# Contrast adjustment of 48 images: tiles of 64 KB rows in three buffers, loads and stores in one written-out order on one queue, sums shared by VectorE and ScalarE

## Chip, cores, metric

One core of a Trainium2 chip. The metric is device time in microseconds (us), the median over executions. The *span* is the time from the first to the last instruction in one profiled execution.

## The reference

```python
x: (16, 3, 512, 512) float32, uniform in [0, 1);  factor = 1.5
mean = np.mean(x, axis=(2, 3), keepdims=True)
return np.clip(mean + factor * (x - mean), 0, 1).astype(np.float32)
```

Each of the 48 images (262,144 pixels, 1 MB) needs its own mean before any of its pixels can be finished. Everything is read once and written once: 50.33 MB in, 50.33 MB out.

## The kernel before

Tiles of four images (4 MB, 128 partitions with rows of 32 KB), the last two tiles of two images, in five buffers. VectorE sums a row, a matmul with a block matrix adds the partitions of an image and multiplies by (1 - factor)/n, ScalarE computes relu(factor * x + bias), VectorE takes the minimum with 1. Loads are issued from SyncE, stores from GpSimd.

```python
TILE_IMGS = [4] * 11 + [2, 2]
X_BUFS = 5
STORE_ENGINE = "gpsimd"
# ... pools, blockw ...
    for i, N in enumerate(TILE_IMGS):
        # ... FREE = columns of this tile, 8192 or 4096; src, dst ...
        nc.sync.dma_start(out=xt, in_=src)
        nc.vector.tensor_reduce(out=rsum, in_=xt, axis=mybir.AxisListType.X, op=mybir.AluOpType.add)
        nc.tensor.matmul(pbias, blockw[N], rsum, start=True, stop=True)
        nc.scalar.copy(out=bias, in_=pbias)
        nc.scalar.activation(out=xt, in_=xt, func=mybir.ActivationFunctionType.Relu, bias=bias, scale=factor)
        nc.vector.tensor_scalar(out=xt, in0=xt, scalar1=1.0, scalar2=None, op0=mybir.AluOpType.min)
        store_eng.dma_start(out=dst, in_=xt)
```

The framework derives the semaphores: a store waits for the last min, a load for the store that last used its buffer.

## Time and profile before

| | before |
|---|---|
| time, median of the first three executions | 240.48 us |
| span of the profiled execution | 238.6 us |
| traffic | 100.66 MB, mean 422 GB/s |
| the two DMA queues | 49.4% + 49.0% of the 16 DMA engines' time |
| VectorE / ScalarE busy | 66% / 37% |

The page of the profile before. In the rows `DMA` and `GB/s` the span is cut into 40 equal slices of 5.97 us; a digit 9 means that the 16 DMA engines were busy for 90% or more of it. The rows `q1` and `q0` are the two DMA queues: packets, MB, share of the engines' time. A group line ends with busy time, the mean duration of one instruction in ns, and the idle time in front of it.

```profile
span 238.6 us, 238 instructions
PE 7.4 (3%) x26; PEld 6.5 (3%) x26; DVE 156.5 (66%) x26; ACT 89.1 (37%) x27; POOL 10.3 (4%) x25
DMA  7999999999999999999999999999999999999995
GB/s 269 434 439 439 439 439 352 439 434 439 439 439 439 439 434 434 423 428 412 423 439 439 434 439 439 439 439 439 434 428 426 426 404 428 431 434 439 428 434 214
...
q1 hardware_dynamic: 1872, 50.33, 49.4%
q0 software_dynamic: 1872, 50.33, 49.0%
...
L77 DVE TENSOR_REDUCE rsum<-xt 128x1 f32<-128x8192 f32 (+1 forms) x13 | 104.4, 8029 | 61.7 <-DMA xt<-in_x_dram 61.7
L90 ACT ACTIVATE xt<-xt,bias 128x8192 f32<-128x8192 f32 (+1 forms) x13 | 85.8, 6598 | 0.4
L97 DVE TENSOR_SCALAR xt<-xt 128x8192 f32<-128x8192 f32 (+1 forms) x13 | 53.2, 4091 | 5.0 <-ACT xt L90 5.0
```

Neither computing engine is near full; the DMA engines are. The timeline of the kernel before shows their pace where stores leave (start, duration of the issue, what; in brackets how long GpSimd had been idle and what ended it):

```profile
136.95 0.53 POOL L104 DMA_DIRECT2D out_dram<-xt  x1 [18.81 <-DVE xt L97]
156.32 0.53 POOL L104 DMA_DIRECT2D out_dram<-xt  x1 [18.84 <-DVE xt L97]
175.69 0.53 POOL L104 DMA_DIRECT2D out_dram<-xt  x1 [18.83 <-DVE xt L97]
```

One store and one load of 4 MB pass every 19.37 us: 433 GB/s. The whole traffic at that pace is 100.66 MB / 433 GB/s = 232.4 us of the 238.6 us span. So the most that any reordering could gain is the rest, 6 us, and part of that (the start, the last landing) can't go. The Trainium skill, "DMA: Bandwidth & Descriptors", section "Where 436 GB/s comes from", gives 435.2 GB/s as the ceiling of the 16 ports that the DMA engines share; the 433 GB/s of this trace agree.

### The profile page before, as it was taken

The page shows a single profiled execution, that of the slowest core. Times are in us where ns is not written, and L with a number is a line of the kernel's source. Part 1 is how long each engine was busy: PE and PEld are TensorE (multiplying, and loading weights), DVE is VectorE, ACT ScalarE, POOL GpSimd, SP SyncE. Part 2 cuts the span into 40 slices and gives each one's busy share as a digit, 9 for nine tenths or more (in the row PEclk, how much of TensorE's full clock was granted, in tenths as well). Part 3 has the DMA queues.
Part 4 walks back from the last instruction along what each step waited for, and adds up shares of the span by engine and source line. Part 5 has one row for each costly group of instructions (what it writes and reads, how often), then busy time and mean ns, then how long its engine had stood idle before and what let it go on. Part 6 is the DMA issues. An engine that isn't in the chain of part 4 may idle for free.

```text
span 238.6 us, 238 instructions
## 1 busy us (share of the span) xinstructions
PE 7.4 (3%) x26; PEld 6.5 (3%) x26; DVE 156.5 (66%) x26; ACT 89.1 (37%) x27; POOL 10.3 (4%) x25
## 2 busy tenths in 40 slices
PE   0000000000000000000000000000000000000000
PEld 0000000000000000000000000000000000000000
DVE  0088999999599079459629909917945979742300
ACT  2002966472906601900920650470190095406000
POOL 2000001000000000000000000000000000500000
DMA  7999999999999999999999999999999999999995
GB/s 269 434 439 439 439 439 352 439 434 439 439 439 439 439 434 434 423 428 412 423 439 439 434 439 439 439 439 439 434 428 426 426 404 428 431 434 439 428 434 214
DMA packets 3744, 100.66 MB, mean 422 GB/s; under 512 B 416, under 2 KB 416, under 8 KB 416
## 3 DMA queue, kind: packets, MB, share of 16 engines
q1 hardware_dynamic: 1872, 50.33, 49.4%
q0 software_dynamic: 1872, 50.33, 49.0%
HBM read 50.33 MB, written 50.33 MB: 422 GB/s over the span
## 4 chain that ended last, share of the span: by engine, by line
issue 38%; DMA 35%; DVE 18%; POOL 2%; POOLq 0%; SPq 0%
DMA xt<-in_x_dram 19%; DMA out_dram<-xt 16%; DVE rsum L77 11%; DVE xt L97 7%; POOL out_dram L104 2%; POOLq L137 0%; SPq L74 0%; POOLq L104 0%
## 5 line engine op out<-in xcount | busy, mean ns | idle before, releaser
L77 DVE TENSOR_REDUCE rsum<-xt 128x1 f32<-128x8192 f32 (+1 forms) x13 | 104.4, 8029 | 61.7 <-DMA xt<-in_x_dram 61.7
L90 ACT ACTIVATE xt<-xt,bias 128x8192 f32<-128x8192 f32 (+1 forms) x13 | 85.8, 6598 | 0.4
L97 DVE TENSOR_SCALAR xt<-xt 128x8192 f32<-128x8192 f32 (+1 forms) x13 | 53.2, 4091 | 5.0 <-ACT xt L90 5.0
L88 ACT COPY bias<-pbias 128x1 f32<-128x1 f32 x13 | 2.1, 160 | 130.6 <-PE pbias L85 130.6
L104 POOL DMA_DIRECT2D out_dram<-xt x13 | 9.0, 692 | 213.0 <-DVE xt L97 212.8
L85 PE MATMUL pbias<-rsum,blockw 128*128 128x1 f32 x26 | 7.4, 355 | 209.5 <-DVE rsum L77 209.5
L85 PEld LDWEIGHTS pbias<-rsum,blockw 128*128 128x128 f32 x26 | 6.5, 311 | 210.3 <-DVE rsum L77 107.1
L88 ACT ACT_TABLE_LOAD x1 | 1.3, 1283 | 0.8 <-PEq L123 0.8
L51 POOL MEMSET blockw<- 32x32 f32 (+1 forms) x6 | 0.8, 128 | 0.2
L49 POOL MEMSET blockw<- 128x128 f32 x2 | 0.3, 205 | 0.3 <-POOLq L123 0.3
L123 POOL MEMSET const-float32-0.0<- 128x1 f32 x1 | 0.1, 104 | 0.2 <-issue 0.2
L123 POOL MEMSET const-bfloat16-1.0<- 128x1 bf16 x1 | 0.1, 113 | 0.0
L123 POOL MEMSET const-uint8-127<- 128x1 uint8 x1 | 0.1, 113 | 0.0
L123 POOL MEMSET const-float32-1.0<- 128x1 f32 x1 | 0.1, 110 | 0.0
## 6 DMA issues: line engine op xcount, KB each, us to landing
xt<-in_x_dram SPq DMA_DIRECT2D x11, 4096.0 KB, 24.6
out_dram<-xt POOLq DMA_DIRECT2D x11, 4096.0 KB, 36.0
xt<-in_x_dram SPq DMA_DIRECT2D x2, 2048.0 KB, 19.5
out_dram<-xt POOLq DMA_DIRECT2D x2, 2048.0 KB, 19.1
```

The lines of the kernel that those rows point to most:

```text
L49: nc.gpsimd.memset(wt, 0.0)
L51: nc.gpsimd.memset(wt[b * PPI : (b + 1) * PPI, b * PPI : (b + 1) * PPI], wconst)
L77: nc.vector.tensor_reduce(out=rsum, in_=xt, axis=mybir.AxisListType.X, op=mybir.AluOpType.add,)
L85: nc.tensor.matmul(pbias, blockw[N], rsum, start=True, stop=True)
L88: nc.scalar.copy(out=bias, in_=pbias)
L90: nc.scalar.activation(out=xt, in_=xt, func=mybir.ActivationFunctionType.Relu, bias=bias, scale=factor,)
L97: nc.vector.tensor_scalar(out=xt, in0=xt, scalar1=1.0, scalar2=None, op0=mybir.AluOpType.min,)
L104: store_eng.dma_start(out=dst, in_=xt)
L123: nc = _bacc.Bacc("TRN2", target_bir_lowering=False, num_devices=1)
```

## The change

The intent: fewer and larger transfers, one queue with an order chosen by hand so that the DMA engines always have the right transfer next, and a tile's sum in half the time. Tiles of 8 MB (128 rows of 64 KB) need 64 KB per partition, and three buffers of them 192 KB, against 160 KB for the five before. The diff, cut to its core:

```diff
-TILE_IMGS = [4] * 11 + [2, 2]
-X_BUFS = 5
-STORE_ENGINE = "gpsimd"
+P = 128
+ROW = 16384
+BUFS = 3
+HALF = ROW // 2
+CHUNK = 4096
+JUNK = 2048
 ...
+    def load(t):
+        xt = xpool.tile([P, ROW], f32, name="xt")
+        nc.sync.dma_start(out=xt, in_=dram(x_f, t))
+        tiles[t] = xt
+
+    def compute(t):
+        xt = tiles[t]
+        n_act = (ROW - HALF) // JUNK
+        sums = rpool.tile([P, 1 + n_act], f32, name="sums")
         nc.vector.tensor_reduce(
-            out=rsum, in_=xt, ...
+            out=sums[:, 0:1], in_=xt[:, 0:HALF], axis=mybir.AxisListType.X, op=Alu.add
         )
+        for j in range(n_act):
+            junk = jpool.tile([P, JUNK], f32, name="junk")
+            a = HALF + j * JUNK
+            nc.scalar.activation(
+                out=junk, in_=xt[:, a : a + JUNK], func=Act.Copy, accum_out=sums[:, 1 + j : 2 + j]
+            )
+        pbias = psum.tile([P, 1], f32, name="pbias")
+        for j in range(1 + n_act):
+            nc.tensor.matmul(pbias, blockw, sums[:, j : j + 1], start=j == 0, stop=j == n_act)
+        bias = bpool.tile([P, 1], f32, name="bias")
+        nc.scalar.copy(out=bias, in_=pbias)
+        for c in range(0, ROW, CHUNK):
+            part = xt[:, c : c + CHUNK]
+            nc.scalar.activation(out=part, in_=part, func=Act.Relu, bias=bias, scale=factor)
+            nc.vector.tensor_scalar(out=part, in0=part, scalar1=1.0, scalar2=None, op0=Alu.min)
+
+    def store(t):
+        nc.sync.dma_start(out=dram(out_f, t), in_=tiles.pop(t))
+
+    for t in range(min(BUFS, n_tiles)):
+        load(t)
+    compute(0)
+    store(0)
+    compute(1)
+    store(1)
+    load(3)
+    compute(2)
+    store(2)
+    load(4)
+    load(5)
+    for t in (3, 4, 5):
+        compute(t)
+        store(t)
```

Below, L0 to L5 and S0 to S5 are the loads and stores of the six tiles. The queue's order is L0 L1 L2 S0 S1 L3 S2 L4 L5 S3 S4 S5. A *turn* is a place in it where a store follows a load or a load follows a store. *Ring* stands below for the list of transfers that one queue hands to the DMA engines.

More of the change, by code (lines that the diff above doesn't have):

```diff
@@ L5 @@
 import concourse.tile as tile
-from concourse import bass_utils, mybir
+from concourse import mybir
 from concourse._compat import with_exitstack
-TILE_IMGS = [4] * 11 + [2, 2]
-X_BUFS = 5
-STORE_ENGINE = "gpsimd"
+P = 128
[4 more added lines that the diff above has]
+JUNK = 2048
 @with_exitstack
@@ L23 @@
     nc = tc.nc
-    P = 128
+    f32 = mybir.dt.float32
+    Alu = mybir.AluOpType
+    Act = mybir.ActivationFunctionType
     B, C, H, W = x.shape
-    n_img = B * C
-    n_pix = H * W
+    n_img, n_pix = B * C, H * W
+    ppi = n_pix // ROW
+    per_tile = P // ppi
+    n_tiles = n_img // per_tile
+    assert ppi * ROW == n_pix and per_tile * n_tiles == n_img
     factor = float(factor)
-    f32 = mybir.dt.float32
-    assert sum(TILE_IMGS) == n_img
-    NMAX = max(TILE_IMGS)
+    wconst = (1.0 - factor) / float(n_pix)
@@ L36, with dram @@
     x_f = x.rearrange("b c h w -> (b c h w)")
     out_f = out.rearrange("b c h w -> (b c h w)")
-    wconst = (1.0 - factor) / float(n_pix)
+    def dram(ap, t):
+        return bass.AP(tensor=ap.tensor, offset=t * P * ROW, ap=[[ROW, P], [1, ROW]])
     consts = ctx.enter_context(tc.tile_pool(name="consts", bufs=1))
-    blockw = {}
-    for N in sorted(set(TILE_IMGS)):
-        wt = consts.tile([P, P], f32, name=f"blockw{N}")
-        PPI = P // N
-        if N == 1:
-            nc.gpsimd.memset(wt, wconst)
-        else:
-            nc.gpsimd.memset(wt, 0.0)
-            for b in range(N):
-                nc.gpsimd.memset(wt[b * PPI : (b + 1) * PPI, b * PPI : (b + 1) * PPI], wconst)
-        blockw[N] = wt
@@ L54 @@
-    xpool = ctx.enter_context(tc.tile_pool(name="xpool", bufs=X_BUFS))
-    rpool = ctx.enter_context(tc.tile_pool(name="rpool", bufs=12))
-    bpool = ctx.enter_context(tc.tile_pool(name="bpool", bufs=12))
-    psum = ctx.enter_context(tc.tile_pool(name="psum", bufs=8, space=bass.MemoryType.PSUM))
-    if STORE_ENGINE == "sync":
-        store_eng = nc.sync
-    elif STORE_ENGINE == "act":
-        store_eng = nc.scalar
-    else:
-        store_eng = nc.gpsimd
-    pix_off = 0
-    for i, N in enumerate(TILE_IMGS):
-        FREE = n_pix * N // P
-        npix_tile = n_pix * N
-        xt = xpool.tile([P, NMAX * n_pix // P], f32, name="xt")[:, :FREE]
-        src = bass.AP(tensor=x_f.tensor, offset=pix_off, ap=[[FREE, P], [1, FREE]])
-        dst = bass.AP(tensor=out_f.tensor, offset=pix_off, ap=[[FREE, P], [1, FREE]])
-        nc.sync.dma_start(out=xt, in_=src)
-        rsum = rpool.tile([P, 1], f32)
+    xpool = ctx.enter_context(tc.tile_pool(name="xpool", bufs=BUFS))
@@ new lines @@
+    jpool = ctx.enter_context(tc.tile_pool(name="jpool", bufs=1))
+    rpool = ctx.enter_context(tc.tile_pool(name="rpool", bufs=2))
+    bpool = ctx.enter_context(tc.tile_pool(name="bpool", bufs=2))
+    psum = ctx.enter_context(tc.tile_pool(name="psum", bufs=2, space=bass.MemoryType.PSUM))
+    blockw = consts.tile([P, P], f32, name="blockw")
+    nc.gpsimd.memset(blockw, 0.0)
+    for a in range(0, P, 2 * ppi):
+        mid, end = a + ppi, a + 2 * ppi
+        nc.gpsimd.memset(blockw[a:end, mid:end], wconst)
+        nc.gpsimd.memset(blockw[a:mid, mid:end], 0.0)
+        nc.gpsimd.memset(blockw[a:mid, a:mid], wconst)
@@ L77 @@
+    tiles = {}
+    def load(t):
[6 more added lines that the diff above has]
+        sums = rpool.tile([P, 1 + n_act], f32, name="sums")
         nc.vector.tensor_reduce(
-            out=rsum,
-            in_=xt,
-            axis=mybir.AxisListType.X,
-            op=mybir.AluOpType.add,
-        )
-        pbias = psum.tile([P, 1], f32)
@@ L85 @@
-        nc.tensor.matmul(pbias, blockw[N], rsum, start=True, stop=True)
-        bias = bpool.tile([P, 1], f32)
-        nc.scalar.copy(out=bias, in_=pbias)
-        nc.scalar.activation(
-            out=xt,
-            in_=xt,
-            func=mybir.ActivationFunctionType.Relu,
-            bias=bias,
-            scale=factor,
-        )
-        nc.vector.tensor_scalar(
-            out=xt,
-            in0=xt,
-            scalar1=1.0,
-            scalar2=None,
-            op0=mybir.AluOpType.min,
-        )
@@ L104 @@
-        store_eng.dma_start(out=dst, in_=xt)
-        pix_off += npix_tile
+            out=sums[:, 0:1], in_=xt[:, 0:HALF], axis=mybir.AxisListType.X, op=Alu.add
+        )
+        for j in range(n_act):
[5 more added lines that the diff above has]
+        pbias = psum.tile([P, 1], f32, name="pbias")
```

## The prediction

> **What bounds the kernel now: the DMA engines.** The slice row "DMA" stands at 9 from the second slice on, and the two queues hold 49.4% and 49.0% of the 16 engines' time. The kernel must move 100.66 MB. In the middle of the timeline stores are issued exactly every 19.37 us, one 4 MB load plus one 4 MB store each: 8.389 MB / 19.37 us = 433 GB/s. At that rate the traffic alone takes 232.4 us of the 238.6 us span. The Trainium skill, "DMA: Bandwidth & Descriptors", section "Where 436 GB/s comes from", puts the ceiling at 435.2 GB/s; the trace agrees. The rest is about 2.3 us of start (first slice 269 GB/s), 3 us of tail (last slice 214 GB/s), and a small dip, for instance slice 7 at 352 GB/s, where the first store joins. VectorE is busy 66%, ScalarE 37%: not the limit.
>
> **What the change does.** The bytes stay. Stores move from GpSimd's queue to SyncE's; the same skill page, "Issuing engines are not separate DMA queues", says both end on the same 16 engines, so no bandwidth is gained. The dips with two queues may go (about 1 us, at most 4 us if every slice reached 439 GB/s). Tiles double to 8 MB, 19.4 us each on the engines, in the queue order L0 L1 L2 S0 S1 L3 S2 L4 L5 S3 S4 S5. Whether the engines ever run dry depends on how long a tile computes.
>
> Costs from the timeline: reduction of 8192 columns 8.69 us; relu 8192 7.12, 4096 3.71, hence 0.83 ns per column and a 2048 sum about 2.0 (four: 8); min of 4096 2.29; matmul pair plus hand-overs about 0.7, five about 2.6. One tile: 8.7 + 2.6 + 0.4 + 4 x 3.6 + 2.4 = 28.5 us. ScalarE per tile about 23, VectorE 17.8, against 38.7 us of DMA per tile in steady state.
>
> **Critical path.** A store comes late at two places. S1 must be issued about 55.6 us after tile 0 lands (three transfers of 19.37, less about 2.5 us for landing notice and start). Two computations take 54 us if the second tile's sums overlap the first's tail, 57 if strictly one after the other: a gap of 0 to 1.5 us. S0 should not be late, unless tile 1's reduction is put before tile 0's last min; then under 1 us. In the middle slack is about 10 us or more (S2, S3). S5 after L4 and L5 has the same 54 to 57 against 55.6: again 0 to 1.5 us. Loads wait for stores already landed while other transfers are queued, so they cost nothing. The faster split reduction lies off the critical path except through these two places.
>
> **Sum:** 238.6 - 1.5 (dips) + 1 (early gap) + 1 (late gap) - about 1 (mixing, short tiles at the end gone) = 237.1 span; the timed runs are 1.9 us above the span: **239.0 us, 80% range 236.0 to 243.0**. Faster by over 2%: 0.11; within 2%: 0.83; slower by over 2%: 0.06.
>
> **What would show it:** the DMA row still 9 nearly everywhere, one hardware queue with about 98%; L3, L4, L5 without a gap ahead of them; at most two shallow dips, near 79 us and near 213 us, where the store's issue waits for VectorE's last min; VectorE's busy time falling by about half of the 104 us of reductions; ScalarE's rising by about 48 us; the chain still mostly DMA.
>
> **What would make it wrong:** large one-direction phases or 64 KB rows running slower (or faster) than the 433 GB/s of mixed 32 KB rows; the scheduler moving a store ahead of a load, or ordering ScalarE and VectorE work so that S1 or S5 is later by several us; accumulating activations costing far more than plain ones.

One remark before the result: the line "Sum" is misadded. Its terms, 238.6 - 1.5 + 1 + 1 - 1, give 238.1 us of span, not 237.1, hence 240.0 us and not 239.0.

## The result, and the profile after

| | before | after |
|---|---|---|
| median of six executions | 240.45 us (239.74 to 240.75) | 241.92 us (241.23 to 242.47) |
| ratio | 1 | 1.0065, interval 1.0042 to 1.0089 |
| span of the profiled execution | 238.6 us | 240.7 us |
| VectorE / ScalarE busy | 156.5 / 89.1 us | 106.9 / 137.0 us |
| DMA queues | two, 98.4% together | one, 98.2% |

Ratios, here and below, are the mean time of one kernel's runs over that of the other's in the same rounds, so not quite the ratio of the medians quoted. Executions over 1.5% slower than the fastest of the same kernel are left out of the means. The time is inside the predicted range and within 2%, but the change made the kernel slower where a small gain was forecast. The outputs are right. The page after, the lines that answer those above:

```profile
span 240.7 us, 323 instructions
PE 13.7 (6%) x60; PEld 13.2 (6%) x60; DVE 106.9 (44%) x30; ACT 137.0 (57%) x79; POOL 1.4 (1%) x17
DMA  9898989899898989899998999999999989898984
GB/s 349 381 490 370 501 349 523 349 523 349 349 523 349 523 349 523 349 468 403 349 490 381 470 403 447 425 436 436 414 447 392 479 381 490 381 490 359 512 359 174
...
q1 hardware_dynamic: 1728, 100.66, 98.2%
...
L93 ACT ACTIVATE xt<-xt,bias 128x4096 f32<-128x4096 f32 x24 | 87.0, 3696 | 0.2
L94 DVE TENSOR_SCALAR xt<-xt 128x4096 f32<-128x4096 f32 x24 | 55.1, 2294 | 61.5 <-ACT xt L93 61.5
L83 ACT ACTIVATE junk<-xt 128x2048 f32<-128x2048 f32 x24 | 45.8, 1908 | 52.3 <-DMA xt<-in_x_dram 51.8
L77 DVE TENSOR_REDUCE sums<-xt 128x1 f32<-128x8192 f32 x6 | 52.1, 8682 | 49.3 <-DMA xt<-in_x_dram 49.3
L83 ACT ACTIVATION_READ_ACCUMULATOR junk<-xt 128x1 f32 x24 | 4.5, 186 | 0.0
```

The computing costs are as forecast: half the reductions (104.4 to 52.1 us), 45.8 us of new sums on ScalarE, plus 0.19 us for each reading of ScalarE's accumulator, which the forecast had not known. The slices swing between 349 and 523 only because a 64 KB packet is booked where it starts, and all 16 engines start one at nearly the same time every 2.42 us; 523 and 349 average to the old pace.

When each transfer was issued, from the timeline of SyncE's queue after (in a line with `x3`, the second number runs from the first issue to the end of the last):

```profile
0.75 1.33 SPq L70 DMA_DIRECT2D xt<-in_x_dram  x3
50.91 28.34 SPq L97 DMA_DIRECT2D out_dram<-xt  x2
81.95 0.34 SPq L70 DMA_DIRECT2D xt<-in_x_dram  x1
106.91 0.33 SPq L97 DMA_DIRECT2D out_dram<-xt  x1
107.33 35.20 SPq L70 DMA_DIRECT2D xt<-in_x_dram  x2
150.90 67.09 SPq L97 DMA_DIRECT2D out_dram<-xt  x3
```

An issue takes about 0.34 us, so S1 was issued near 78.9 us and S5 near 217.7 us: the two late places that the prediction had named. In the trace's packet records S1's first packets start at about 80.9 us, directly after S0's last ones, so S1 left no gap. S5 did. The windows of the changed kernel around it follow. A window line gives its stretch and length, the busy time of each computing engine, the granted clock, and as its last two numbers the DMA share and GB/s; a packet is booked whole where it starts, so a share can exceed 1. 66 GB/s in 1 us is one packet of 65,536 bytes (here the last one of S4 on the engine furthest behind), 983 GB/s is 15 of them:

```profile
217.00:218.00 1.00, 0.00 (x0) 0.00 (x0) 0.63 (x1) 0.00 (x0) 0.00 (x0) 1.00 0.15 66
218.00:219.00 1.00, 0.00 (x0) 0.00 (x0) 0.00 (x0) 0.00 (x0) 0.00 (x0) 1.00 2.30 983
```

15 of 16 engines start S5 in the same microsecond although they had been spread out before. By the packet records ten of them had ended S4 before any packet of S5 started, and so waited for it; the mean wait over all 16 was 0.3 us. The engine that was furthest behind starts alone, at 219.9 us, and it ends last.

There is a second loss. A window of 2.4 us that holds exactly one packet of each engine reads 437 GB/s (16 x 65,536 bytes / 2.4 us), and its share times 2.4 us is then the mean time of one packet. The last packets of L2, just ahead of S0, in the changed kernel (first and second line), and in the kernel before the time around its first store with windows of 1.2 us for packets of 32 KB:

```profile
55.00:57.40 2.40, 0.00 (x0) 0.00 (x0) 2.40 (x1) 1.55 (x2) 0.00 (x0) 1.00 1.01 437
57.40:59.80 2.40, 0.27 (x2) 0.28 (x2) 2.07 (x1) 0.00 (x0) 0.00 (x0) 1.00 1.51 437
```

```profile
36.00:37.20 1.20, 0.00 (x0) 0.00 (x0) 1.20 (x1) 1.20 (x1) 0.67 (x1) 1.00 1.01 437
37.20:38.40 1.20, 0.00 (x0) 0.00 (x0) 1.20 (x1) 1.20 (x1) 0.00 (x0) 1.00 1.09 437
38.40:39.60 1.20, 0.00 (x0) 0.00 (x0) 1.20 (x1) 1.00 (x1) 0.00 (x0) 1.00 1.47 437
```

After: 1.01 x 2.4 = 2.42 us for an ordinary packet, 1.51 x 2.4 = 3.62 us for the packets at the turn, 1.2 us lost on all engines. Before: (0.08 + 0.46) x 1.2 = 0.65 us lost, once. The changed kernel repeats it at a later turn, L3 to S2 (shown further down).

### The profile page after: what moved, and what is told of

Its sections match the earlier page's. It is cut to its first block, busy times and chain, and to the rows that moved or that the text cites. A ratio compares the mean times of both kernels' runs of the same rounds, so it can differ in the third digit from the quotient of the medians.

```text
span 240.7 us, 323 instructions
## 1 busy us (share of the span) xinstructions
PE 13.7 (6%) x60; PEld 13.2 (6%) x60; DVE 106.9 (44%) x30; ACT 137.0 (57%) x79; POOL 1.4 (1%) x17
## 3 DMA queue, kind: packets, MB, share of 16 engines
q1 hardware_dynamic: 1728, 100.66, 98.2%
## 4 chain that ended last, share of the span: by engine, by line
DMA 39%; ACT 23%; DVE 17%; another core or an unknown queue 4%; PE 4%; ACTq 1%; issue 1%; DVEq 0%; SPq 0%
DMA xt<-in_x_dram 26%; ACT xt L93 23%; DVE sums L77 14%; DMA out_dram<-xt 13%; PE pbias L88 4%; DVE xt L94 3%; ACTq L143 1%; ACT bias L90 0%; DVEq L77 0%; DVEq L94 0%; SPq L70 0%
## 5 line engine op out<-in xcount | busy, mean ns | idle before, releaser
L93 ACT ACTIVATE xt<-xt,bias 128x4096 f32<-128x4096 f32 x24 | 87.0, 3696 | 0.2
L94 DVE TENSOR_SCALAR xt<-xt 128x4096 f32<-128x4096 f32 x24 | 55.1, 2294 | 61.5 <-ACT xt L93 61.5
L83 ACT ACTIVATE junk<-xt 128x2048 f32<-128x2048 f32 x24 | 45.8, 1908 | 52.3 <-DMA xt<-in_x_dram 51.8
L77 DVE TENSOR_REDUCE sums<-xt 128x1 f32<-128x8192 f32 x6 | 52.1, 8682 | 49.3 <-DMA xt<-in_x_dram 49.3
L88 PE MATMUL pbias<-sums,blockw 128*128 128x1 f32 x60 | 13.7, 354 | 186.8 <-DVE sums L77 186.8
L88 PEld LDWEIGHTS pbias<-sums,blockw 128*128 128x128 f32 x60 | 13.2, 329 | 187.2 <-DVE sums L77 155.7
L90 ACT COPY bias<-pbias 128x1 f32<-128x1 f32 x6 | 1.0, 159 | 25.0 <-PE pbias L88 25.0
L83 ACT ACTIVATION_READ_ACCUMULATOR junk<-xt 128x1 f32 x24 | 4.5, 186 | 0.0
L63 POOL MEMSET blockw<- 16x16 f32 x4 | 0.4, 104 | 0.2
L64 POOL MEMSET blockw<- 16x16 f32 x4 | 0.4, 104 | 0.0
```

The costliest lines, as they stand in the source:

```text
L63: nc.gpsimd.memset(blockw[a:mid, mid:end], 0.0)
L64: nc.gpsimd.memset(blockw[a:mid, a:mid], wconst)
L77: nc.vector.tensor_reduce(out=sums[:, 0:1], in_=xt[:, 0:HALF], axis=mybir.AxisListType.X, op=Alu.add)
L83: nc.scalar.activation(out=junk, in_=xt[:, a : a + JUNK], func=Act.Copy, accum_out=sums[:, 1 + j : 2 + j])
L88: nc.tensor.matmul(pbias, blockw, sums[:, j : j + 1], start=j == 0, stop=j == n_act)
L93: nc.scalar.activation(out=part, in_=part, func=Act.Relu, bias=bias, scale=factor)
```

## The experiments

Three theories were written down first. **A**: a turn from loads to stores within one ring costs about 1.2 us by itself. **B**: S1 and S5 are issued late and leave gaps. **C**: rows of 64 KB are slower. The kernels of one batch ran on one chip and share their runs of the kernel before; each has six executions, e1 and e2 five, e12 four.

| run | what | median us | ratio to before (95% interval) |
|---|---|---|---|
| e3_copy_same_order | same transfers, nothing computed | 240.65 | 1.0010 (0.9971 to 1.0048) |
| e4_copy_grouped | copy, 3 turns | 239.34 | 0.9956 (0.9926 to 0.9987) |
| e5_copy_alternating | copy, 9 turns | 241.29 | 1.0038 (0.9993 to 1.0082) |
| e7_half_rows | changed, all transfers halved | 239.72 | 0.9975 (0.9943 to 1.0006) |
| after_again | changed, unaltered | 241.86 | 1.0073 (1.0053 to 1.0094) |
| e1_stores_gpsimd | changed, stores on GpSimd's queue | 255.12 | 1.0633 (1.0607 to 1.0658) |
| e2_stores_act | changed, stores on ScalarE's queue | 253.43 | 1.0558 (1.0534 to 1.0581) |
| e8_copy_alternating_half | copy, 9 turns, halved | 241.11 | 1.0043 (1.0016 to 1.0069) |
| e9_half_stores | changed, stores halved | 239.72 | 0.9971 (0.9950 to 0.9992) |
| e10_half_loads | changed, loads halved | 239.50 | 0.9962 (0.9939 to 0.9984) |
| e11_grouped_small | 4 MB tiles, six loads, six stores, twice | 239.62 | 0.9965 (0.9945 to 0.9986) |
| e12_late_last_store | changed, S5 3.3 us later | 244.63 | 1.0175 (1.0149 to 1.0201) |
| e13_early_last_store | changed, S5 earlier | 241.68 | 1.0063 (1.0030 to 1.0097) |
| e14_copy_same_half_stores | copy, stores halved | 239.68 | 0.9999 (0.9972 to 1.0026) |
| e15_copy_same_again | as e3 | 239.65 | 0.9990 (0.9972 to 1.0007) |
| e16_only_first_two_late | copy, but S0 and S1 as late as in the changed kernel | 241.60 | 1.0070 (1.0047 to 1.0092) |
| e17_second_store_early | changed, S1 and S5 earlier | 239.68 | 0.9999 (0.9969 to 1.0030) |
| after_third | changed, unaltered | 241.10 | 1.0044 (1.0028 to 1.0061) |

The batches are e3 to e7; after_again, e1, e2, e8; e9 to e12; e13 to e15; e16, e17, after_third. The kernel before had medians from 239.79 to 240.46 us in these batches, so comparisons across batches can be off by up to 0.3%; closer ones are made inside a batch.

### 1. The transfers alone

All computing is taken out, so the results are wrong (a copy). Only the order is written differently:

```diff
-    for t in range(min(BUFS, n_tiles)):
-        load(t)
-    compute(0)
-    ...
+    for what in "L0 L1 L2 S0 S1 L3 S2 L4 L5 S3 S4 S5".split():            # e3
+    for what in "L0 L1 L2 S0 S1 S2 L3 L4 L5 S3 S4 S5".split():            # e4
+    for what in "L0 L1 S0 L2 S1 L3 S2 L4 S3 L5 S4 S5".split():            # e5
+        (load if what[0] == "L" else store)(int(what[1:]))
```

> The same six loads and six stores in the same order on SyncE's queue, all computation taken out (the result is wrong on purpose: a copy); a store waits only for its load. Theory A (a turn from loads to stores inside one ring costs about 1.2 us; the changed kernel has three): nothing computed was in the way, so about the changed kernel's time, 241.6 us (241.0 to 242.3), with the three slow packets still there. Theory B (S1 and S5 are issued late because computing takes too long): the gaps go, 238.5 to 239.5 us. Theory C (64 KB rows are slower everywhere): 241.6 us too, but without slow packets at the turns.

> The same copy, order L0 L1 L2 S0 S1 S2 L3 L4 L5 S3 S4 S5: two turns from loads to stores and one back, in place of three and two. A: 1.2 to 2.2 us less than the copy in the changed kernel's order, near 240 us. B and C: the same time as that copy.

> The same copy, order L0 L1 S0 L2 S1 L3 S2 L4 S3 L5 S4 S5: five turns from loads to stores and four back. A: 2.4 to 4.4 us more than the copy in the changed kernel's order, 244 to 246 us. B and C: the same time as that copy.

The copy in the changed kernel's own order took 240.65 us, between what A and B had expected. The number of turns pushes the time the way A says, 239.34, 240.65 and 241.29 us for 3, 5 and 9 turns, but later turns cost far less than 1.2 us: e5 missed A's 244 to 246 us, and its six executions scatter from 239.79 to 242.78 us. In all three profiles the packets at the *first* turn from loads to stores took 0.9 to 1.3 us more than ordinary ones, as a mean over all engines, and at the later turns only those of some engines were slow. A is too simple: the first turn costs about 1 us, the others a part of it.

The most important reading is another. Even with nothing computed, this order gains nothing on the kernel before: 1.001 (0.9971 to 1.0048). This order with one queue and long rows has no credit to give that these runs could resolve. The grouped order e4, with three turns, was 0.4% faster.

### 2. The same kernel in smaller transfers

```diff
-        nc.sync.dma_start(out=xt, in_=dram(x_f, t))
+        for c in (0, HALF):
+            nc.sync.dma_start(out=xt[:, c : c + HALF], in_=dram(x_f, t)[:, c : c + HALF])
```

and the same for the stores.

> The changed kernel with every load and store cut into two of 128 rows of 32 KB, order and computation as they were. A: turns as before, 241.9 us (241.2 to 242.6). B: the first half of S1 and S5 can leave about 7 us earlier, so the gaps go: 239 to 240 us. C: rows of 32 KB as in the kernel before: 239 to 240 us.

239.72 us and correct: A missed, B or C could be right. To tell them apart, the alternating copy was halved too, and the changed kernel was run again beside it:

> The alternating copy (five turns from loads to stores, four back; 241.3 us with 64 KB rows, ratio to before 1.004) with each load and store cut into two of 32 KB rows; result wrong on purpose. If the turns cost the same whatever the row (A alone): ratio about 1.004 again. If the cost of a turn, or how far the engines drift apart, goes with the size of a packet (C in its narrower form): ratio 0.996 to 0.999, as the changed kernel gained from half rows.

> The changed kernel once more, unaltered. In its first profile the last packets before the turns from loads to stores took 3.3 to 3.9 us in place of 2.42, at L2-S0 and L3-S2 on all 16 engines, at L5-S3 and S1-L3 on some. If the turns are the cause by themselves (A), the same turns stall again by about the same, 241.9 us (241.2 to 242.5). If which turn stalls is chance, the stall at L3-S2 may be gone while L2-S0 stays, and the time moves with it by about 1 us.

The halved copy had 1.0043, like the copy with 64 KB rows (1.0038). Halving rows does not make turns cheaper, and C is out. The changed kernel repeated at 1.0073. The stall at L3-S2 was weaker this time (2.74 us a packet, against 3.50 us in the first profile), and the time was the same: in this profile the engines waited 0.9 us on average for S5 instead.

### 3. A second ring

```diff
-        nc.sync.dma_start(out=dram(out_f, t), in_=tiles.pop(t))
+        nc.gpsimd.dma_start(out=dram(out_f, t), in_=tiles.pop(t))      # e1;  nc.scalar for e2
```

> The changed kernel with the stores issued from GpSimd's queue, as in the kernel before; tiles, rows and computation as changed. A (a turn inside one ring stalls; two rings that alternate packet by packet do not): one stall left where the first store joins, 238.5 to 239.5 us, and no slow packets at later turns. C (rows of 64 KB are at fault, not the single ring): unchanged, 241.2 to 242.5 us.

> As the run with stores on GpSimd's queue, but on ScalarE's queue, which is a hardware queue as SyncE's is. A: the same 238.5 to 239.5 us, since it is the second ring that matters and not who fills it; ScalarE's own work shifts by the wait for the last min, 2.4 us a tile, which is in no one's way except at the end. C: 241.2 to 242.5 us.

A clear miss of both theories: 255 and 253 us. The slices of the run with stores on GpSimd's queue (6.32 us each) show why:

```profile
DMA  8979999799979988979989999799897998303993
GB/s 332 498 332 498 415 415 498 332 394 436 498 332 498 404 373 384 498 342 487 477 353 498 415 416 498 332 498 446 384 498 342 487 477 353 166 0 166 498 498 166
```

There is a hole at slices 35 to 37 (215 to 234 us). With two rings a store and a load that are both waiting share the engines, so the loads land later; the last reduction began at 202.12 us against 189.54 us in the changed kernel, the last store was issued at 230.51 us, and the engines had run dry by then. The single ring with its written order lets the next load have all 16 engines. In e2 something else is added: ScalarE worked through tile 2's first sums, which had to wait for L2 until 70.15 us, before it copied tile 1's bias (72.06 us, against 61.86 us in the changed kernel), so S1 left only at 90.94 us. How much of e2's loss is due to that was not separated. The Trainium skill, "DMA: Bandwidth & Descriptors", section "Issuing engines are not separate DMA queues", says that all queues end on the same engines and interleave; that agrees. What it doesn't say is that a second queue can cost 6%, as in this kernel with its three buffers (their number was not varied). These two runs say nothing for or against turns.

### 4. The late last store

```diff
 # e9: store() issues two transfers of 32 KB rows;  e10: load() does
 # e12:
         nc.scalar.copy(out=bias, in_=pbias)
+        for _ in range(2 if t == 5 else 0):
+            junk = jpool.tile([P, JUNK], f32, name="junk")
+            nc.scalar.activation(out=junk, in_=xt[:, 0:JUNK], func=Act.Relu, bias=bias, scale=factor)
 # e11:
-ROW = 16384
-BUFS = 3
+ROW = 8192
+BUFS = 6
+    for g in range(0, n_tiles, BUFS):
+        for t in range(g, g + BUFS):
+            load(t)
+        for t in range(g, g + BUFS):
+            compute(t)
+            store(t)
```

> The changed kernel with each store cut into two of 128 rows of 32 KB; loads whole. The first half of S5 can now leave after two chunks of the last relu, about 7 us earlier, so that the engines no longer wait for it. Theory B2 (in the changed kernel 14 or 15 of the 16 engines start S5 together when it is issued, which sets a floor of about 238.0 us of span): the floor goes, ratio to before 0.997 to 1.001. Theory A2 (only the engines that stalled most at the turns decide, and they never waited for S5): ratio 1.005 to 1.009, as the changed kernel.

> The changed kernel with each load cut into two of 32 KB rows; stores whole, so S5 leaves after the last min as before, but VectorE may begin its half of the sums before the second half has landed, which brings S5 forward by several us. B2: ratio 0.997 to 1.001. A2: 1.005 to 1.009.

> The changed kernel with two more activations of 2048 columns on ScalarE (3.8 to 4.0 us, result unused) after the bias of the last tile: S5 is issued about 3.9 us later, nothing else moves. B2: most engines waited for S5 already, the slowest had about 1.2 us of slack, so the time grows by 2.4 to 3.9 us: 244.2 to 245.8 us, ratio 1.017 to 1.024. If S5's issue has slack of several us: no change, ratio 1.005 to 1.009.

> The changed kernel with tiles of 4 MB (rows of 32 KB), six buffers (the same memory) and the order six loads, six stores, six loads, six stores on SyncE's queue: two turns from loads to stores and one back, and 20 us or more of slack for the computing of the last tile of each six. Both theories: no wait for a last store, few stalls, the engines end within 1 us of each other; ratio 0.994 to 0.998, about 239.3 us, better than both kernels. If rows of 32 KB or more stores cost something not seen so far: above 1.000.

B2 is the theory that the wait for S5 sets the changed kernel's time, A2 that the stalls at the turns do. e9 and e10, at 0.9971 and 0.9962, came out as B2 said (e10 even a little below its range). e11, at 0.9965, was within what both theories allowed and decides nothing. e12 came out at 244.63 us (four executions): S5 issued 3.3 us later than in the first profile (220.9 against 217.7 us) cost 2.4 to 3.1 us by the ratios, across batches. The windows of e12 show all 16 engines waiting for it and then starting together (1049 GB/s is 16 packets):

```profile
219.00:220.00 1.00, 0.00 (x0) 0.00 (x0) 1.00 (x1) 0.00 (x0) 0.00 (x0) 1.00 0.00 0
220.00:221.00 1.00, 0.00 (x0) 0.00 (x0) 0.89 (x1) 0.00 (x0) 0.00 (x0) 1.00 0.00 0
221.00:222.00 1.00, 0.00 (x0) 0.00 (x0) 0.00 (x0) 0.00 (x0) 0.00 (x0) 1.00 2.45 1049
```

So S5 has almost no slack in the changed kernel. That looked like the answer, but e9 and e10 move more than S5: they also let S1 leave earlier. The direct test moves S5 alone, by leaving half of the last tile unfinished (wrong), and two copies ask what halving does by itself:

```diff
-        for c in range(0, ROW, CHUNK):
+        for c in range(0, HALF if t == 5 else ROW, CHUNK):             # e13
```

> The changed kernel with the last two of the four relu and min chunks of the last tile left out (its result wrong on purpose): S5 is issued 7 us earlier, all transfers and all else as they were. If the late S5 is all of it (B2): ratio 0.996 to 0.999, as with half stores. If it is part, and the rest are stalls at the turns of whole rows: ratio 0.9995 to 1.004, as in the copy of the same order (1.001). If S5 has no part: 1.005 to 1.009.

> The copy in the changed kernel's order (nothing computed, wrong on purpose) with each store cut into two of 32 KB rows. If halving cures stalls at the turns: ratio 0.995 to 0.998, under that of the whole copy run beside it by 0.003 or more. If halving only let S5 leave earlier: no difference from the whole copy.

> The copy in the changed kernel's order with whole transfers, once more, for the comparison with half stores on the same chip: ratio 0.998 to 1.004, as before (1.001).

B2 falls: with S5 issued near 209.9 us, all transfers whole, the ratio was still 1.0063. Its fastest execution (239.64 us) was below any of the changed kernel in its three batches (lowest 240.84), its slowest (242.87) above all of them. The late S5 is at most a floor under the good executions; on average its removal gained nothing that could be resolved. And halving the stores alone is worth nothing: 0.9999 against 0.9990 for the whole copy beside it.

### 5. The second store

What e3, e7, e9, e10, e14 and e15 have in common, and the changed kernel, e12 and e13 have not, is that S1 or its first half is issued several microseconds before the engines reach it (in e10 at 76.1 us, in the copies before 45 us, against 78.9 us). The new theory **D**: S1's late issue makes the engines stall at turns that come later, although it leaves no gap of its own.

```diff
 # e16: only tiles 0 and 1 are computed, the others are copied (wrong on purpose)
-    compute(2)
     store(2)
     load(4)
     load(5)
     for t in (3, 4, 5):
-        compute(t)
         store(t)
 # e17: half of tiles 1 and 5 unfinished (wrong on purpose); four unused activations keep S2's time
+        for _ in range(4 if t == 2 else 0):
+            junk = jpool.tile([P, JUNK], f32, name="junk")
+            nc.scalar.activation(out=junk, in_=xt[:, 0:JUNK], func=Act.Relu, bias=bias, scale=factor)
-        for c in range(0, ROW, CHUNK):
+        for c in range(0, HALF if t in (1, 5) else ROW, CHUNK):
```

> Tiles 0 and 1 computed as in the changed kernel (S0 issued near 50.9 us, S1 near 78.9), tiles 2 to 5 only copied (wrong on purpose). If S1's late issue (theory D) makes the engines stall at S1-L3 and L3-S2: ratio 1.003 to 1.008, and those stalls of 0.3 to 1.1 us a turn in the profile. If not: as the plain copy, 0.998 to 1.002, and only the first turn stalls on all engines.

> The changed kernel with half of tile 1's and half of tile 5's relu and min left out (wrong on purpose), so S1 and S5 are issued about 7 us earlier, and four activations added to tile 2 so that S2 is issued when it was, near 107 us. Against the run with S5 alone early (1.0063) only S1 is moved. D: the stalls at S1-L3 and L3-S2 go, ratio 0.996 to 1.000. If S1 is innocent: 1.003 to 1.008, stalls as before.

> The changed kernel, unaltered, on the chip of these two: ratio 1.005 to 1.009; stalls on all 16 engines at L2-S0, on some or all at S1-L3, L3-S2 and L5-S3.

Three kernels on one chip: 1.0070, 0.9999, 1.0044. The intervals of e16 and e17 do not overlap, that of the changed kernel touches e17's; five of e17's six executions took 239.4 to 239.8 us (the sixth 241.68 us), all of the other two 240.84 us or more. The issues of S0 and S1, from the timelines of SyncE's queue in e16 and then in e17: S1 leaves at 78.9 and at 71.5 us.

```profile
50.86 28.35 SPq L97 DMA_DIRECT2D out_dram<-xt  x2
```

```profile
50.71 21.15 SPq L100 DMA_DIRECT2D out_dram<-xt  x2
```

And the windows at the turn L3 to S2, one packet of each engine in each: an ordinary packet, and the one at the turn. In order, the changed kernel (its first profile), e16, e17, and the copy e15:

```profile
114.20:116.60 2.40, 0.00 (x0) 0.00 (x0) 0.00 (x0) 0.00 (x0) 0.00 (x0) 1.00 1.01 437
116.60:119.00 2.40, 0.00 (x0) 0.00 (x0) 0.00 (x0) 0.00 (x0) 0.00 (x0) 1.00 1.46 437
```

```profile
114.20:116.60 2.40, 0.00 (x0) 0.00 (x0) 0.00 (x0) 0.00 (x0) 0.00 (x0) 1.00 1.01 437
116.60:119.00 2.40, 0.00 (x0) 0.00 (x0) 0.00 (x0) 0.00 (x0) 0.00 (x0) 1.00 1.39 437
```

```profile
114.20:116.60 2.40, 0.00 (x0) 0.00 (x0) 0.00 (x0) 0.00 (x0) 0.00 (x0) 1.00 1.01 437
116.60:119.00 2.40, 0.00 (x0) 0.00 (x0) 0.00 (x0) 0.00 (x0) 0.00 (x0) 1.00 1.04 437
```

```profile
114.20:116.60 2.40, 0.00 (x0) 1.00 1.01 437
116.60:119.00 2.40, 0.00 (x0) 1.00 1.07 437
```

The packets at this turn took 1.46 x 2.4 = 3.50 us in the changed kernel, 3.34 us in e16, 2.50 us in e17 and 2.57 us in the copy. Computing is not the cause: e16 computes nothing after S1 and stalls, e17 computes to the end and doesn't, and S2 is issued at 82 us in e16 and at 107 us in e17. The stall at the first turn is no different in the two (1.1 and 1.3 us). e16 and e17 differ in S5's issue too, but e13 had S5 early and S1 late, and stalled. Against e13, on another chip, e17 moves S1 alone: 1.0063 and 0.9999.

The other traces agree. The second window, 116.60 to 119.00 us, has a share of 1.14 to 1.46 in all six profiles with S1 issued at 78.7 to 78.9 us (the changed kernel three times, e12, e13, e16), and of 1.02 to 1.08 in all seven others with this order in one queue, where S1 or its first half left by 76.2 us (e3, e7, e9, e10, e14, e15, e17). In e10 whole stores and all computing are in place, S1 left at 76.1 us, and the share is 1.05. D holds. *Why* an issue 2 us ahead of its turn makes packets some 40 us later slow, no run here shows; it stays open. S1 early with S5 late was not run. An estimate from the traces: the changed kernel issued S5 56.1 us after its reduction of tile 4 began (161.5 to 217.7 us); in e17 that reduction began at 159.5 us, so S5 would be issued near 215.6 us and start 0.8 us later, as in the changed kernel, near 216.4 us, which is about when the engines of e17 reached it (216.2 to 217.1 us).

## Why the prediction was right or wrong

1. **What bounds the kernel: right.** One queue at 98.2% after, two at 98.4% before; a copy without any computing is no faster (0.999 and 1.001).
2. **"239.0 us": wrong in sign.** The forecast was 0.6% faster, measured 0.65% slower, 2.9 us apart. One microsecond of that is the misaddition in the line "Sum"; its terms make 240.0 us.
3. **The step that failed is "- 1.5 (dips)" together with "- about 1 (mixing, short tiles at the end gone)".** These runs show no such credit of 2.5 us. Without either late store, e17 took 0.9999 of the time before (0.9969 to 1.0030, so at most 0.7 us less), the copies in this order 0.9990 and 1.0010; even e10, the fastest version that computes, gained only 0.9 us (0.9962; at most 1.5 us by its interval). The dip where the first store joins was taken for a fault of having two queues. It is there with one ring too, and larger: 0.65 us before, 1.2 us after.
4. **"S1 ... a gap of 0 to 1.5 us": right place and about the right size, wrong mechanism.** S1 was issued at 78.9 us, against the 78.3 us that the prediction's own figures allow (22.7 + 55.6), and no gap followed. The cost came later, as stalls at S1-L3 and L3-S2, which the prediction did not have; that the size still fits is luck. On one chip the two kernels with a late S1 were 0.45% and 0.71% slower than e17, 1.1 to 1.7 us (e17 has S5 early too; moving S5 alone gained nothing that could be resolved).
5. **"S5 ... again 0 to 1.5 us": the wait was there, its worth was not.** Ten of 16 engines waited for S5, 0.3 us as a mean over all, but the one furthest behind, by its stalls, did not wait and ended last. Taking the wait away alone left 1.0063; making it 3.3 us longer cost 2.4 to 3.1 us.
6. **The sum with what the runs showed:** 238.6 + 0 (credit) + 1.1 to 1.7 (S1) + 0 (S5) + 1.9 (from span to timed run) = 241.6 to 242.2 us; measured 241.92. The terms were measured after the fact, so this shows that they fit together and is no independent test.
7. **"L3, L4, L5 without a gap ahead of them", "VectorE's busy time falling by about half of the 104 us", "ScalarE's rising by about 48 us": right** (52.1 us of reductions left; 89.1 to 137.0 us).

The version to keep: e10, e11, e9 and e7 are correct and take 239.5 to 239.7 us, 1.4 to 2.4 us less than the changed kernel's 241.1 to 241.9 us. e10 was also 0.38% faster than the kernel before beside it (0.9939 to 0.9984). On other chips the kernel before itself took 239.8 us, so this last margin is small. The Trainium skill, "Perfetto Trace Analysis", section "DMA Optimizations", says that splitting transfers may let some start sooner; e9 and e10 agree, though the copies e14 and e15 show that splitting the stores has no worth except through the earlier issue.

## What to carry to other kernels

When the DMA engines are already at 98%, first ask a copy with the same transfers what the new order could gain at best; here the answer, nothing that could be resolved, would have corrected the forecast's credit. With one queue and few buffers, count for each store how long before its turn it is issued, and try cutting transfers in two where that is only a microsecond or two, as it was here (78.9 against 80.9 us): a late store can cost time without any gap ahead of it. And measure before adding a second queue to a hand-written order; in this kernel, with three buffers, it cost about 6%.

## What the Trainium skill lacked or had wrong

- "DMA: Bandwidth & Descriptors" has no cost for a change from loads to stores: the packets at the first such turn took 3.62 us in place of 2.42 us on all 16 engines in the changed kernel, and 0.65 us were lost once in the kernel before with its two queues.
- The same page has no figure for how far ahead of its turn a transfer should be issued. A store issued at 78.9 us, 2 us ahead, brought stalls of 0.3 to 1.1 us (mean over the engines) at a turn near 118 us in six profiles; issued at 71.5 us it did not (ratios 1.0070 and 0.9999).
- The same page, section "Rules for kernel authors", says that spreading transfers over several issuing engines "doesn't help". It can hurt: moving the stores to a second queue took 5.6% and 6.3% more than the kernel before, because loads then share the engines with stores and land later (with the stores on GpSimd's queue the last reduction began at 202.12 us in place of 189.54 us).
- No page found gives the cost of reading ScalarE's accumulator: 24 readings of 186 ns here, one after each summing activation. The activation itself agrees with "ScalarE: Activation LUTs", section "What ACT_TABLE_LOAD costs": 186 ns + 0.833 ns per column gives 1.89 us for 2048 columns as an estimate, measured 1.91 us.
